# Low weight parts of layer 0's output projection on another engine, and two more pauses in the latent stream's routing

## The chip, the cores and the metric

The kernel runs on one core of a Trainium2 chip. A core has a matrix engine (TensorE, PE in the profile), a vector engine (VectorE, DVE), an activation engine (ScalarE, ACT), a general engine (GpSimd, POOL) and a queue engine that starts most DMAs (SyncE, SP). Each engine works through its own list of instructions in order; semaphores make one wait for another. The metric is device time in microseconds (us) of one execution, the median of several runs.

## The reference

The reference is a block of two layers for a stream x of 256 latent tokens and a stream ctx of 256 context tokens, each token 1024 wide, float32. Cut to what matters here, a layer is:

```python
x = x + g1 * merge_branches(attn_x, conv_x, pool_x, gate_x, lp)       # ... @ lp['w_out'] at its end
if not last:
    ctx = ctx + cg1 * merge_branches(attn_c, conv_c, pool_c, gate_c, lp)
x = x + g2 * expert_choice_ffn(modulate(rmsnorm(x, norm2_g[l]), sh2, sc2), w_router[l], ...)
if not last:
    ctx = ctx + cg2 * expert_choice_ffn(modulate(rmsnorm(ctx, ...), csh2, csc2), w_router[l], ...)

def expert_choice_ffn(h, w_router, w_gate, w_up, w_down):
    aff = softmax(h @ w_router)                    # 16 experts
    g, idx = top_k(transpose(aff), cap)            # each expert takes its 32 best tokens
    xe = h[idx]
    ye = (silu(xe @ w_gate) * (xe @ w_up)) @ w_down * g
    return zeros_like(h).at[idx].add(ye)
```

In layer 1, the last, only x goes on after the attention's keys and values.

## The kernel before

The work of a layer comes in two parts. The mixer (input projection, attention, convolution, pooling, three merges) ends with the merged sum m, eight pieces of 128x512 in layer 0 (both streams side by side) and of 128x256 in layer 1. Then come the output projection with w_out, the routing and the experts, whose weights, 2 MB at a time, fill nearly all of the DMA's time.

Products of this part keep float32 precision with two halves of each operand in the fast format: a high part h, rounded by ScalarE, and a low part, the rest, from a subtraction. `split` makes both for 128x1024 weights: `L238` is ScalarE's copy, `L239` the subtraction, which goes to VectorE for the letter "v" and to GpSimd for "p". The table `LOW` holds one letter per layer for each weight; for `wout` it is "pv": GpSimd in layer 0, VectorE in layer 1. The halves lie in the tile `ws`, of which there are two buffers here, so ScalarE can fill one only when TensorE is done with the one before the last.

`project(s)` forms stream s's output projection in ten steps: for each half of the columns four blocks of 12 products (`L872`: 4 of m's high part mh with the weights' high part, 4 of m's low part ml with it, 4 of mh with the weights' low part), and then the gate multiply (`L877`, VectorE) and the addition to the stream (`L879`: GpSimd for one of the four pieces, VectorE for three) with its squares (`L880`). The gates are first spread over the partitions by two products (`L853`). After each block and after each half it pauses (`yield`).

`route(s)` is the routing of stream s: products of the router with the first half of the columns (transposes `L895`, copies to `xT`, products `L904`), a pause, the second half, a pause; then the scale of the norm on GpSimd (`L909`, `L207`, `L208`), the logits' copy `lg` and transposes (`L915`), the softmax on VectorE and ScalarE (`L917` to `L931`), its transposes (`L934`), four rounds that find the eight largest values and strike them out (`L942`, `L943`), a pause; then the mask `mk`, the places of the chosen tokens by products with triangular matrices (`L954` to `L972`), the one-hot matrices S (`L965`, scaled by ScalarE in `L968`), and a last pause. Its tiles in the matrix accumulator come from a pool of four, `ax`.

`gather` multiplies a stream with S (`L987`) and so picks each expert's tokens (`xeT`). `L1080` is an expert's first pair of products, `L1103` and `L1108` its last, `L1125` the addition back.

The order of the work is set by these pauses: a loop runs one generator and lets another go on by one piece at each pause. In layer 0, x's routing starts after the sixth step of x's projection and goes on after its last; after that one piece of it follows each step of ctx's projection, and ctx's own routing starts after the sixth of those. The build's scheduler then places the instructions of each engine by that order and by priority; splits have a raised one, so they stand some steps ahead.

```python
        rt = route(0)
        for i, _ in enumerate(project(0)):
            if i == 5:
                next(rt)
        next(rt)
        rt1 = route(1) if NS == 2 else None
        if NS == 2:
            for i, _ in enumerate(project(1)):
                next(rt, None)
                if i == 5:
                    next(rt1)
```

Of the kernel before, what the change touches and what calls it, by code (L numbers as in the profile page):

```python
# [24 lines left out]


TAPS = dict(attn=(1, 4), pool=(4, 0), merge0=(8, 1), merge2=(9, 18))
LOW = dict(q="vv", k="pv", v="pv", cg="vv", ca="vv", pu="pv", g0="vv", g1="pv", g2="vp", wo="vv", wout="pv")
PSCALE = ("avaa", "aaaa")
MOD_EVERY = (1, 2)  # L30
MOD_AHEAD = 1
# [96 lines left out]
def dit_block(ctx: ExitStack, tc: tile.TileContext, out, kcv, kb16, rope_in, tok, cols, w_mod0, w_mod,  # L128
# [16 lines left out]
    def bank(tag, dt=F32):  # L145
        pool, bufs = psum[tag]
        return pool.tile([128, 512], dt, tag=tag, name=tag, bufs=bufs)
# [19 lines left out]
    def t2(name, n=512, dt=F32):  # L167
        return L.tile([128, n], dt, tag="t2", name=name, bufs=6)
# [42 lines left out]
    for l in range(DEPTH):  # L211
        last = l == DEPTH - 1
        NS = 1 if last else 2
# [256 lines left out]
        def pump_taps(n):  # L470
            for _ in range(min(n, len(taps))):
                ch, k = taps.popleft()
                if k == 0:
                    nc.vector.tensor_scalar(acc[:, ch], up[:, ch, :, 0:256], dw[:, ch:ch + 1],
                                            vec[:, VCB + 4 * l + ch:VCB + 4 * l + ch + 1],
                                            op0=ALU.mult, op1=ALU.add)
                else:
                    nc.vector.scalar_tensor_tensor(acc[:, ch], up[:, ch, :, k:k + 256],  # L478
                                                   dw[:, 4 * k + ch:4 * k + ch + 1], acc[:, ch],
                                                   op0=ALU.mult, op1=ALU.add)  # L480
# [20 lines left out]
        def unit(src, n, view="p (k n) -> p k n", eng="v", **kw):  # L501
            w = split(src, view, eng, **(kw or dict(k=8)))
            w = [v.rearrange("p (k n) -> p k n", k=8) for v in w]
            ps = bank("mm")
            mm3(ps[:, :n], w, (hh, hl), 8, n)
            nunit[0] += 1
            if nunit[0] % MOD_EVERY[l] == 0:
                pump_mod()
            return ps

        def win(c0):
            return load(w_in[l, c0 // 256], "p (k n) -> p k n", k=8)
# [20 lines left out]
        for u in range(2):  # L533
            tv = qw.pop() if qw else qload(u)
            for v in range(2):
                i = 2 * u + v
                ps = unit(tv[:, :, :, 64 * v:64 * v + 64], N, "p (k h n) -> p k h n",
                          LOW["q"][l], k=8, h=2)
                qx = t2("qx", N)
# [13 lines left out]
        kvw = win(OK_)  # L553
        ps = unit(kvw[:, :, 0:128], 512, eng=LOW["k"][l])
        kf = t2("kf")
        roped(kf[:, 0:256], ps)
        nc.scalar.activation(kf[:, 256:512], ps[:, 256:512], AF.Copy)
        for kv in range(2):
# [4 lines left out]
            nc.vector.tensor_sub(KL[ho, kv, :], kf[hp], KS[hp, kv, :].bitcast(F32))  # L563
        ps = unit(kvw[:, :, 128:256], 512, eng=LOW["v"][l])
        vf = t2("vf", 512)
# [93 lines left out]
        def sv(ap):  # L659
            return ap.rearrange("p (s n) -> p s n", s=NS)  # L660

        def conv_units():
            for u in range(2):
                wg_, wa_ = win(OG + 256 * u), win(OA + 256 * u)
                for v in range(2):
                    ch = 2 * u + v
                    ps = unit(wg_[:, :, 128 * v:128 * v + 128], N, eng=LOW["cg"][l])
                    th = t2("th", N)
                    nc.scalar.activation(th, ps[:, :N], AF.Tanh, scale=0.5)
                    yield  # L670
                    ps = unit(wa_[:, :, 128 * v:128 * v + 128], N, eng=LOW["ca"][l])
                    nc.vector.scalar_tensor_tensor(up[:, ch, :, CPAD:CPAD + 256], sv(th), 1.0,
# [30 lines left out]
        for u in range(2):  # L703
            wz = win(OP + 256 * u)
            for v in range(2):
                g = 2 * u + v
                w = POOLW[g]
                ps = unit(wz[:, :, 128 * v:128 * v + 128], N, eng=LOW["pu"][l])
                pump_taps(TAPS["pool"][l])
# [174 lines left out]
        def route(s):  # L884
# [25 lines left out]
            r = rms_scale(ss, 2)  # L910
            lg = t2("lg", 384)
            nc.vector.tensor_copy(lg, pl[:, 0:384])
            pt = bank("ax")
            for t in range(3):
                nc.tensor.transpose(pt[:, t * 128:(t + 1) * 128], lg[:, t * 128:(t + 1) * 128], ident)  # L915
# [13 lines left out]
            nc.vector.reduce_sum(sm, ex, axis=AX.X)  # L929
            nc.vector.reciprocal(sm, sm)  # L930
            nc.vector.tensor_mul(ex, ex, sm.unsqueeze(2).to_broadcast([128, 2, NE]))  # L931
            pa = bank("ax")
            for t in range(2):
                nc.tensor.transpose(pa[0:NE, t * 128:(t + 1) * 128], ex[:, t, :], ident)  # L934
# [62 lines left out]
        if last:  # L997
            prefetch(1)
# [8 lines that stand above are left out]
# [26 lines left out]
        for e in range(NE):  # L1033
# [36 lines left out]
            for i in range(4):  # L1070
                wg, wu = [eload().rearrange("p (k n) -> p k n", k=2) for _ in range(2)]
                for kk in range(2):
                    k = 2 * i + kk
# [126 lines left out]
```

## Time and profile before

| | us |
|---|---|
| median of 3 runs | 1696.55 (1694.93 to 1698.94) |
| profiled execution | 1699.61 |
| its span in the profile | 1697.8 |
| TensorE busy, of the span | 1469.8 |
| VectorE busy | 673.0 |
| ScalarE busy | 407.1 |
| GpSimd busy | 231.1 |

The DMA moves 530 MB in the span, 312 GB/s on the mean, and about 428 GB/s where it is full. In the chain of work that ended last, TensorE has 38% of the span, the DMA 27% and VectorE 4%.

### The profile page before, as it was taken

To read this page: it belongs to the slowest core of one execution; us is meant where nothing else is said; L and a number is where in the kernel's file an instruction comes from. 1 tells how busy PE (TensorE), PEld (TensorE's weight loads), DVE (VectorE), ACT (ScalarE), POOL (GpSimd) and SP (SyncE) were. 2 spreads that over 40 slices of the span, in tenths; PEclk is the share of its full clock that TensorE was granted. 3 is DMA by queue.
4 is the path that set the end of the run, shared out by engine and by line. 5 is a ranking of instruction groups with operands and counts; after the bars stand their busy time and mean duration, and the time that the engine had idled before them with its cause. 6 is when DMAs were issued, how large, how long until landed. Compare 5 with 4: busy or idle time off the path is not lost.

```text
span 1697.8 us, 19127 instructions
## 1 busy us (share of the span) xinstructions
PE 1469.8 (87%) x7788; PEld 797.6 (47%) x7788; DVE 673.0 (40%) x1141; ACT 407.1 (24%) x760; POOL 231.1 (14%) x234
## 2 busy tenths in 40 slices
PE   6999989999899999999988899999978656666575
PEld 2666667888654433333332377789843111111111
DVE  3589983441652221121211378966532110111011
ACT  3466212232432100100000258334421000000001
POOL 0301610254730000000000020225100000000000
PEclk9999999999999999999999999999989886887878
DMA  9644445243447999999999765665699999999995
GB/s 398 235 174 140 142 172 180 99 184 138 173 177 302 428 425 428 428 426 428 428 426 427 304 239 184 220 251 202 248 387 428 427 428 428 428 427 428 428 428 240
DMA packets 48185, 530.01 MB, mean 312 GB/s; under 512 B 5345, under 2 KB 6113, under 8 KB 7906
## 3 DMA queue, kind: packets, MB, share of 16 engines
q1 hardware_dynamic: 46224, 526.10, 76.2%
q10 hardware_dynamic: 1874, 2.70, 0.5%
q8 instruction: 61, 1.00, 0.2%
q14 instruction: 26, 0.21, 0.0%
HBM read 527.73 MB, written 1.05 MB: 311 GB/s over the span
## 4 chain that ended last, share of the span: by engine, by line
PE 38%; DMA 27%; DVE 4%; issue 2%; ACT 1%; POOL 1%; POOLq 0%; ACTq 0%; DVEq 0%; SPq 0%
DMA we<-in_w_e_dram 24%; PE mm L1080 11%; PE mm L1103 6%; PE mm L987 3%; PE mm L872 3%; PE mm L497 2%; PE mm L496 2%; PE mm L499 2%; DMA A<-in_w_e_dram 2%; PE ax L1125 2%; DVE acc L478 1%; PE mm L1108 1%; PE ax L1095 1%; PE md L255 1%; DVE ws L239 1%
## 5 line engine op out<-in xcount | busy, mean ns | idle before, releaser
L1080 PE MATMUL mm<-we,xeT 128*32 128x512 f32 (+1 forms) x1880 | 348.0, 662 | 99.5 <-DMA we<-in_w_e_dram 99.5
L1080 PEld LDWEIGHTS mm<-we,xeT 128*32 128x32 f32 (+1 forms) x1880 | 94.8, 129 | 342.2 <-issue 186.6
L496 PE MATMUL mm<-hh,ws 128*128 128x512 f32 (+1 forms) x672 | 222.8, 350 | 0.2
L497 PE MATMUL mm<-hl,ws 128*128 128x512 f32 (+1 forms) x672 | 219.7, 345 | 0.8 <-DVE hl L430 0.8
L238 ACT ACTIVATE ws<-w 128x1024 fp32r<-128x1024 f32 x132 | 139.4, 1058 | 301.0 <-PE mm L499 192.8
L1087 DVE TENSOR_TENSOR hm<-si,mm 64x512 f32<-64x512 f32 x48 | 33.1, 690 | 413.0 <-ACT si L1085 272.3
L1085 ACT ACTIVATE si<-mm 64x512 f32<-64x512 f32 x48 | 28.3, 590 | 686.7 <-PE mm L1080 686.7
L478 DVE SCALAR_TENSOR_TENSOR acc<-up,dw,acc 128x512 f32<-128x512 f32 (+1 forms) x240 | 154.5, 685 | 1.1
L239 DVE TENSOR_TENSOR ws<-w,ws 128x1024 fp32r<-128x1024 f32 x94 | 124.6, 1329 | 66.9 <-ACT ws L238 66.4
L496 PEld LDWEIGHTS mm<-hh,ws 128*128 128x128 f32 x672 | 128.3, 192 | 28.9 <-issue 12.6
L497 PEld LDWEIGHTS mm<-hl,ws 128*128 128x128 f32 x672 | 128.2, 191 | 18.6 <-issue 3.5
L499 PE MATMUL mm<-hh,ws 128*128 128x512 f32 (+1 forms) x672 | 132.5, 339 | 0.7 <-DVE ws L239 0.6
L239 POOL TENSOR_TENSOR ws<-w,ws 128x1024 fp32r<-128x1024 f32 x38 | 95.8, 2527 | 203.6 <-ACT ws L238 124.3
L1103 PE MATMUL mm<-we,hT 128*64 128x512 f32 x432 | 111.0, 637 | 4.8 <-ACT hT L1098 4.8
L499 PEld LDWEIGHTS mm<-hh,ws 128*128 128x128 f32 x672 | 107.2, 189 | 15.2 <-DVE ws L239 1.4
L1045 POOL COPY sel<-kc 48x128 f32<-48x128 f32 (+1 forms) x16 | 4.6, 285 | 798.2 <-DVE hm L1087 427.3
L1115 DVE TENSOR_TENSOR Y<-mm,G 32x512 f32<-32x512 f32 x64 | 44.0, 687 | 132.3 <-PE mm L1103 131.5
L1108 PE MATMUL mm<-we,hT 128*32 128x512 f32 x424 | 70.2, 779 | 9.4 <-DMA we<-in_w_e_dram 6.3
L1103 PEld LDWEIGHTS mm<-we,hT 128*64 128x64 f32 x432 | 33.6, 146 | 76.0 <-issue 65.3
L1125 PE MATMUL ax<-Y,sg 128*128 128x512 f32 x128 | 58.4, 603 | 8.8 <-DVE Y L1118 6.4
L1095 PE MATMUL ax<-kc,hm 64*128 64x64 f32 x192 | 32.6, 295 | 30.9 <-DVE hm L1087 30.2
L1118 DVE TENSOR_TENSOR Y<-mm,G 64x512 f32<-64x512 f32 x32 | 22.0, 689 | 94.0 <-PE mm L1108 93.6
(261 smaller groups left out, 1708.0 us busy)
## 6 DMA issues: line engine op xcount, KB each, us to landing
we<-in_w_e_dram SPq DMA_DIRECT2D x166, 2048.0 KB, 27.1
w<-in_w_mod_dram SPq DMA_DIRECT2D x44, 1024.0 KB, 5.4
w<-in_w_in_dram SPq DMA_DIRECT2D x42, 1024.0 KB, 4.8
A<-in_w_e_dram SPq DMA_DIRECT2D x20, 2048.0 KB, 23.8
w<-in_w_out_dram SPq DMA_DIRECT2D x12, 1024.0 KB, 4.9
we<-in_w_e_dram SPq DMA_DIRECT2D x10, 1024.0 KB, 17.2
wm<-in_w_mod_dram SPq DMA_DIRECT2D x4, 1024.0 KB, 19.1
w<-in_w_attn_o_dram SPq DMA_DIRECT2D x4, 1024.0 KB, 4.8
```

The costliest lines, as they stand in the source:

```text
L238: nc.scalar.activation(h, src, AF.Copy)
L239: (nc.gpsimd if eng == "p" else nc.vector).tensor_sub(lw, src, h.bitcast(F32))
L478: nc.vector.scalar_tensor_tensor(acc[:, ch], up[:, ch, :, k:k + 256], dw[:, 4 * k + ch:4 * k + ch + 1], acc[:, ch], op0=ALU.mult, op1=ALU.add)
L496: nc.tensor.matmul(ps, wh[:, k, :], ah[:, k, :n], start=k == 0, stop=False)
L497: nc.tensor.matmul(ps, wh[:, k, :], al[:, k, :n], start=False, stop=False)
L499: nc.tensor.matmul(ps, wl[:, k, :], ah[:, k, :n], start=False, stop=k == nk - 1)
L872: nc.tensor.matmul(pss[t], a, b, start=k == 0 and st == 0, stop=k == 7 and st == 2)
L987: nc.tensor.matmul(px, XS[s][:, t, paired(d)], Sv, start=t == 0, stop=t == 1)
L1080: nc.tensor.matmul(o, xeT[k // 4][:, k % 4, e, :], w[:, kk, 512 * f:512 * f + 512], start=k == 0, stop=k == 7)
L1103: nc.tensor.matmul(pd[64 * h:64 * h + 64, :], hT[:, 64 * k:64 * k + 64], rhs, start=k == 0, stop=k == 7)
L1108: nc.tensor.matmul(pd[o:o + 32, :], hT[:, c0:c0 + 32], rhs, start=k < 2, stop=k >= 6)
L1125: nc.tensor.matmul(po, sgs[s][:, t * 128:(t + 1) * 128], Y[:, s, cols], start=True, stop=True)
```

## The change

The letter for `wout` in layer 0 becomes "v", and `route` pauses twice more, after the copy of the logits and after the softmax. The two pauses hold only for a stream that is not the last of its layer (`s < NS - 1`): x in layer 0. In layer 1 there is one stream, so nothing moves there. The loop over `project(1)` is as before, so x's routing after its second pause now takes four steps of ctx's projection instead of two, each followed by a block of ctx's products.

```diff
-LOW = dict(q="vv", k="pv", v="pv", cg="vv", ca="vv", pu="pv", g0="vv", g1="pv", g2="vp", wo="vv", wout="pv")
+LOW = dict(q="vv", k="pv", v="pv", cg="vv", ca="vv", pu="pv", g0="vv", g1="pv", g2="vp", wo="vv", wout="vv")
...
             lg = t2("lg", 384)
             nc.vector.tensor_copy(lg, pl[:, 0:384])
+            if s < NS - 1:
+                yield
             pt = bank("ax")
...
             nc.vector.tensor_mul(ex, ex, sm.unsqueeze(2).to_broadcast([128, 2, NE]))
+            if s < NS - 1:
+                yield
             pa = bank("ax")
```

From here on a line in the changed program stands 2 lower after the first pause and 4 lower after the second. All 16 subtractions of layer 0's w_out leave GpSimd's list and stand in VectorE's. VectorE's list from the maximum of the softmax (`rmx`) to the first rounds of the top eight (`wk`), before:

```order
L924 TENSOR_REDUCE rmx<-rl_3427 128x2
L926 TENSOR_TENSOR rex<-rl_3427,rmx 128x32
L929 TENSOR_REDUCE rsm<-rex 128x2
L930 RECIPROCAL rsm<-rsm 128x2
L931 TENSOR_TENSOR rex<-rex,rsm 128x32
L942 MAX m_3444<-ax 16x8
L943 MATCH_REPLACE wk<-m_3444,ax 16x256
L942 MAX m_3444<-wk 16x8
```

The same place of VectorE's list in the changed program, where `ws` is a split's low part and `tmp` ctx's gate multiply:

```order
L239 TENSOR_TENSOR ws<-w,ws 128x1024
L926 TENSOR_REDUCE rmx<-rl_3442 128x2
L928 TENSOR_TENSOR rex<-rl_3442,rmx 128x32
L931 TENSOR_REDUCE rsm<-rex 128x2
L932 RECIPROCAL rsm<-rsm 128x2
L933 TENSOR_TENSOR rex<-rex,rsm 128x32
L239 TENSOR_TENSOR ws<-w,ws 128x1024
L946 MAX m_3476<-ax 16x8
L947 MATCH_REPLACE wk<-m_3476,ax 16x256
L877 TENSOR_TENSOR tmp<-mm,gb 128x512
L946 MAX m_3476<-wk 16x8
L239 TENSOR_TENSOR ws<-w,ws 128x1024
```

What stood in one piece is now laid between splits and gate multiplies; one more split, a gate multiply and two additions follow before the last round. TensorE's list from the transposes of the logits (`lg`) to those of the softmax (`rex`), before:

```order
L915 MATMUL ax<-kc,lg 128x128 x3
L872 MATMUL mm<-ws,mh 128x512 x2
L872 MATMUL mm<-ws,ml 128x512 x4
L872 MATMUL mm<-ws,mh 128x512 x4
L934 MATMUL ax<-kc,rex 16x128 x2
```

and the same place in the changed program:

```order
L917 MATMUL ax<-kc,lg 128x128 x3
L872 MATMUL mm<-ws,mh 128x512 x4
L872 MATMUL mm<-ws,ml 128x512 x4
L872 MATMUL mm<-ws,mh 128x512 x6
L938 MATMUL ax<-kc,rex 16x128 x2
```

There are 14 of ctx's products between the two where there were 10. TensorE's list from there to the transposes of the struck-out values (`wk`), before:

```order
L872 MATMUL mm<-ws,mh 128x512 x4
L872 MATMUL mm<-ws,ml 128x512 x4
L872 MATMUL mm<-ws,mh 128x512 x8
L872 MATMUL mm<-ws,ml 128x512 x4
L872 MATMUL mm<-ws,mh 128x512
L948 MATMUL ax<-kc,wk 128x16 x2
```

and in the changed program:

```order
L872 MATMUL mm<-ws,mh 128x512 x2
L872 MATMUL mm<-ws,ml 128x512 x4
L872 MATMUL mm<-ws,mh 128x512 x8
L872 MATMUL mm<-ws,ml 128x512 x4
L872 MATMUL mm<-ws,mh 128x512 x8
L872 MATMUL mm<-ws,ml 128x512 x4
L872 MATMUL mm<-ws,mh 128x512 x8
L872 MATMUL mm<-ws,ml 128x512 x2
L952 MATMUL ax<-kc,wk 128x16 x2
```

Here 40 products stand between, where 21 stood. The rest of x's routing, up to S, comes correspondingly later among ctx's products.

## Rows read from the trace of the kernel before

**Rows 1.** Stretches: length, busy PE, PEld, DVE, ACT, POOL, clock, DMA share, GB/s
```profile
424.50:455.20 30.70, 28.12 (x134) 20.05 (x133) 19.07 (x14) 14.42 (x22) 22.43 (x10) 1.00 0.63 240
455.20:490.60 35.40, 31.87 (x161) 22.83 (x160) 17.91 (x36) 13.87 (x23) 21.55 (x12) 0.95 0.30 99
...
501.00:517.40 16.40, 15.07 (x74) 8.38 (x75) 9.35 (x30) 6.25 (x16) 0.00 (x0) 1.00 0.00 2
...
560.00:788.00 228.00, 216.60 (x936) 78.16 (x938) 47.04 (x72) 18.02 (x33) 1.15 (x4) 0.96 1.01 427
```
**Rows 2.** Waits of the DMA queue SP, 490 to 560: total us, times, longest
```profile
SPq L355 <- PE mm L1080: 51.0, 8, 26.3
```
**Rows 3.** Chain that ended last, layer 0's experts: start, length
```profile
795.17 29.59 DMA we<-in_w_e_dram
```
**Rows 4.** TensorE in order of time: start, span; idle before in brackets
```profile
457.51 0.51 PE L895 MATMUL ax<-kc,xr 128*128 128x128 f32 x2 [0.83 <-POOL xr L879]
...
462.95 0.49 PE L915 MATMUL ax<-kc,lg 128*128 128x128 f32 x3
463.19 0.71 PE L872 MATMUL mm<-ws,mh 128*128 128x512 f32 x2
...
467.92 0.38 PE L934 MATMUL ax<-kc,rex 128*16 128x128 f32 x2 [2.17 <-DVE rex L931]
468.05 1.55 PE L872 MATMUL mm<-ws,mh 128*128 128x512 f32 x4
...
473.41 1.07 PE L872 MATMUL mm<-ws,ml 128*128 128x512 f32 x4
...
475.71 0.27 PE L972 MATMUL ax<-bt,mk 128*16 128x256 bf16 x1
...
481.40 0.99 PE L895 MATMUL ax<-kc,xc 128*128 128x128 f32 x6 [0.53 <-DVE xc L879]
...
489.72 1.07 PE L872 MATMUL mm<-ws,mh 128*128 128x512 f32 x4
490.63 1.88 PE L987 MATMUL mm<-S,xr 128*128 128x512 f32 x4
...
513.81 6.66 PE L1080 MATMUL mm<-we,xeT 128*64 128x512 f32 x30
```
**Rows 5.** GpSimd in order of time
```profile
441.60 2.38 POOL L239 TENSOR_TENSOR ws<-w,ws 128x1024 fp32r<-128x1024 f32 x1 [0.69 <-ACT ws L238]
```
**Rows 6.** VectorE in order of time; the last row is layer 1's
```profile
440.95 0.69 DVE L879 TENSOR_TENSOR xr<-xr,tmp 128x512 f32<-128x512 f32 x1
...
442.28 2.24 DVE L879 TENSOR_TENSOR xr<-xr,tmp 128x512 f32<-128x512 f32 x1
...
463.95 2.47 DVE L921 SCALAR_TENSOR_TENSOR rl<-rls,rstd 128x16 f32<-128x16 f32 x2
...
468.74 0.42 DVE L942 MAX8 m<-ax 16x8 f32<-16x256 f32 x1 [0.97 <-ACT slaff L937]
...
469.71 0.42 DVE L942 MAX8 m<-wk 16x8 f32<-16x256 f32 x1
...
499.36 0.38 DVE L921 SCALAR_TENSOR_TENSOR rl<-rls,rstd 128x16 f32<-128x16 f32 x2
...
1213.16 1.23 DVE L239 TENSOR_TENSOR ws<-w,ws 128x1024 fp32r<-128x1024 f32 x1 [1.49 <-ACT ws L238]
```
**Rows 7.** VectorE's groups by form, 424.5 to 490.6: busy us, mean ns
```profile
L827 DVE TENSOR_TENSOR ml<-A,mh 128x512 fp32r<-128x512 f32 x8 | 14.0, 1805 | 6.8 <-ACT mh L826 6.8
```
**Rows 8.** Stretches again: layer 1's output projection of x
```profile
1204.70:1230.70 26.00, 26.00 (x134) 19.91 (x132) 14.82 (x20) 11.85 (x20) 0.78 (x1) 1.00 0.63 264
```
**Rows 9.** Stretches again: behind the softmax
```profile
469.40:471.10 1.70, 1.70 (x5) 1.32 (x4) 1.58 (x5) 0.00 (x0) 1.12 (x1) 0.50 0.00 0
```
**Rows 10.** ScalarE in order of time
```profile
476.51 1.06 ACT L238 ACTIVATE ws<-w 128x1024 fp32r<-128x1024 f32 x1 [2.72 <-PE mm L872]
477.47 1.32 ACT L968 ACTIVATE S<-S,rstd 128x512 f32<-128x512 f32 x2
```

## The prediction

> **What bounds the kernel now.** I read the stretches first, since the change touches one place: the end of layer 0's mixer. From 424.5 to 490.6 us TensorE forms the output projection of both streams and the first routing; from there to 513.8 it gathers tokens; then the experts start. The reader is to see three things. In the two stretches of the projection (424.5 to 455.2 the latent stream x, 455.2 to 490.6 the context stream ctx with x's routing laid between) TensorE is the engine with the most work, 28.1 of 30.7 and 31.9 of 35.4 us, and the DMA is not full [rows 1]. From 501.0 to 517.4 the DMA moves nothing: the expert buffers are filled, and the queue waits, up to 26.3 us at a time, for an expert product to free one [rows 1, 2]. From 560 on it is full, and later the chain consists of waits for expert weights, such as 29.6 us at 795 [rows 1, 3]. So layer 0 ends when a full DMA stream ends, but that stream starts when TensorE begins its first expert, at 513.81 [rows 4]. Whatever the projection gains should move the stream, and all behind it, by the same amount. The order of the DMAs on SP is the same before and after.
>
> **The change part by part.** Durations are those of the profiled execution, 1699.61 us (span 1697.8 and 1.8 around it); the runs shown have a median of 1696.55, 3.06 lower, and I take the gain off that.
>
> *Low parts of w_out on VectorE.* The change takes 16 subtractions of 128x1024 off GpSimd, 2.38 us each when undisturbed [rows 5], and adds 16 to VectorE, where layer 1 already does them at 1.23 us [rows 6]: 19.7 us on top of the 37.0 (19.07 + 17.91) that VectorE is busy in the two stretches [rows 1]. But part of the 37.0 is waiting inside instructions. While GpSimd subtracts from 441.60 to 443.98, VectorE's add at 442.28 takes 2.24 us, where the same form at 440.95 takes 0.69; a 128x16 multiply-add pair at 463.95 takes 2.47, against 0.38 for the other stream's pair at 499.36 [rows 5, 6]; and the eight subtractions on the merged sum take 1.8 us on average [rows 7]. With GpSimd out of the way that gives back 8 x (1.8 - 0.69) = 8.9 us, 1.6 at the add and 2.1 at the pair, so VectorE ends near 44 us of work in some 58.
>
> For x's products I need no model, because layer 1 has the same program there: one stream, the same products, the same interleaving of the first half of the routing, and the low parts on VectorE. That stretch takes 26.0 us with TensorE busy in all of it [rows 8], against 30.7 here [rows 1]: **4.7 us**. What differs is that the merged sum's subtractions are 128x512 here, twice layer 1's size. If half of each of the 8 lay on the path, 8 x 0.35 = 2.8 us, only 1.9 would be gained; I keep that as the low end. They should be hidden: the later ones are first needed in the third block of 12 products, 24 x 0.227 = 5.4 us after the first (0.227 is the step from 489.72 to 490.63 over four products [rows 4]).
>
> *ctx's products with x's routing between, and the two pauses.* Before, TensorE passes from the logits' transposes at 462.95 over 10 products to the transposes of the softmax at 467.92, for which it waits 2.17 us [rows 4]. The chain between, from the end of the first transposes, is 4.5 us. Without the blocked pair it is 2.1 shorter; with the one split that now stands in it on VectorE it is 1.23 longer: 3.6. The first pause gives 14 products as cover, 3.2 us, and a change-over of 0.1, so 0.3 of the 2.17 stays: 1.9 gained. Behind that wait the granted clock is 0.50 (the 1.2 GHz level) from 469.4 to 471.1 [rows 9], and the 16 products from 468.05 to 473.41 take 5.36 us instead of 16 x 0.227 = 3.6 [rows 4]; less a change-over, 1.6 is gained if the clock stays. The wait of 0.83 at 457.51 left it at 1.00 up to 468 or so, so 0.3 should leave it too; that wait itself, for GpSimd's add on x, I leave as it is. The wait of 0.53 at 481.40 is for an add on ctx that a GpSimd split had blocked; it goes: 0.5 gained. Together 4.0.
>
> Against that stand three costs. The second pause lays 40 products (9.1 us) between the softmax's transposes and those of the top-8 result, where 21 lay. But on VectorE the four rounds of MAX8 and MATCH_REPLACE8, 0.97 each (468.74 to 469.71) [rows 6], now have three splits (3.7) and three gate operations of 0.69 between them: 3.9 + 3.7 + 2.1 = 9.7. I charge 0.5. TensorE changes between products and transposes some two times more, 0.1 each (two products after transposes take 0.71 at 463.19, where 0.39 + 0.23 is the bare time): 0.2. And the one-hot matrix S, ready at 478.8 for a gather at 490.63 [rows 4, 10], loses nearly all of its 12 us of lead. From the last mask product (475.98) S took 2.8 us; in the new order 10 products (2.3) and 24 small routing products and transposes stand between, over 4 us in all. I charge nothing; a late S would cost what is missing, 1 us or so. The stretch then gives 4.0 - 0.7 = **3.3 us**, between 0 and 5.5.
>
> The sum is 4.7 + 3.3 = **8.0 us**: 1691.6 against the profiled execution, 1688.6 against the median. GpSimd keeps two adds and the norm's scale, so its own queue holds up nothing new. The stretch from 490.6 to 513.8 has the same instructions as before and no split in it.
>
> One rule weighs against part of this. The add at 442.28 shows the later of the two engines held until the other's instruction is over [rows 5, 6]. The Trainium skill ("SBUF — State Buffer", section "SBUF: two separate sides") states that the port pair which VectorE and GpSimd share is an exclusive lock, that it goes to whichever starts first, and that a VectorE operation with two SBUF inputs takes it; the trace agrees with 2.24 against 0.69. By that rule VectorE's splits can now hold GpSimd's remaining add on x, which TensorE awaits at 457.51, by up to 1.23 us: the time would be 1689.8.
>
> **The rivals.** (a) *Only x's stretch gains.* VectorE serves the routing and the splits in one order, so ctx's stretch wins as much as it loses: 4.7, time 1691.9. For it: the top-k chain of 9.7 against 9.1. Against it: the 2.17 wait and the slow clock behind it have a cause that goes. (b) *The weights' stream takes it back*: 1696.5. For it: the DMA is full from 560 on and has the chain's longest parts. Against it: it is idle for 16 us first, waiting for this very TensorE. (c) *Slower: VectorE's order.* There are six places, from the logits to the mask, where a split stands behind a routing instruction that waits for TensorE or ScalarE, while only two split buffers exist. If at each TensorE had to wait for a whole split, 1.06 on ScalarE [rows 10] and 1.23 on VectorE, it would lose 6 x 2.29 = 13.7, so 13.7 - 8.0 = 5.7 us slower: 1702.3. It decides from 8.0 / 6 = 1.3 us at each place. Against it: the low half is needed only after 8 of a block's 12 products, 1.8 us after the high half, and in layer 1 VectorE stands idle 1.49 us for ScalarE before a split while TensorE is never late [rows 6, 8]. (d) *All small waits go*, also the top-k's, the one at 457.51 and the change-overs: 10.5 us, 1686.0.
>
> **How the numbers follow.** The forecast (a gain of 6 to 10) gets 0.66, (a) with 3 to 6 0.16, (b) 0.08, (c) 0.05, (d) 0.05. A gain of 10.5 with 0.5 for the spread of a median gives 1685.5; the low end of x's stretch with 0.6 from ctx's, a gain of 2.5, gives 1694.0. About 0.2%, 3.4 us, is what a measurement tells from no change. Of (a) 0.13 lies beyond it: faster 0.66 + 0.05 + 0.13 = 0.84, same 0.03 + 0.08 = 0.11, slower 0.05.
>
> **What would show it.** In the profile after: x's stretch 26 us long with VectorE's splits at 1.23; no VectorE add above 1 us there; a wait for the softmax under 0.5 and the granted clock at 1.00 throughout; the gather beginning near 482.6 and the first expert near 505.8; the DMA's idle stretch before it, and the expert stretch, as long as now. A split that comes late at several blocks, a gather waiting for S, or a first expert that comes earlier without the end moving would make the prediction wrong.

## The result, and the profile after

| | before | after |
|---|---|---|
| median of the runs made for the comparison | 1697.18 (1694.93 to 1700.23, 5 runs) | 1688.83 (1687.23 to 1690.28, 5 runs) |
| profiled execution | 1699.61 | 1690.28 |
| its span | 1697.8 | 1688.5 |

The changed kernel takes 0.9945 of the time before, with a 95% interval of 0.9932 to 0.9957: faster by 0.55% by this ratio, while the two medians differ by 8.3 us (0.49%). 1688.6 was predicted, between 1685.5 and 1694.0. A later run of the same changed kernel, in another comparison, gave 1691.34 against 1700.00, again 0.9945 [0.9934, 0.9957].

The stretches of the output projection (length, then busy time of PE, PEld, DVE, ACT and POOL with instruction counts, granted clock, DMA share, GB/s), and part of the DMA's idle stretch behind it. The first begins with the first product of the projection (`L853`), the second with the gate multiply that follows x's last product (`L877`; 455.20 us before, 450.74 after), and the second ends at the gather:

```profile
424.69:450.74 26.05, 26.05 (x133) 20.12 (x132) 19.08 (x23) 14.40 (x22) 1.68 (x1) 1.00 0.74 282
450.74:482.21 31.47, 30.81 (x162) 22.00 (x161) 21.70 (x43) 13.97 (x23) 2.37 (x4) 1.00 0.45 158
505.00:508.00 3.00, 3.00 (x17) 1.20 (x17) 0.41 (x1) 1.77 (x3) 0.00 (x0) 1.00 0.00 0
```

Beside [rows 1]: cut at the same events, x's stretch went from 30.68 (424.52 to 455.20) to 26.05 us, which is layer 1's length [rows 8], ctx's from 35.43 (to 490.63) to 31.47. GpSimd's 44 us of work in the two stretches has become 4. VectorE has 15 of the 16 splits more in them (the first runs ahead of them, at 423.31) and yet only 40.8 us of work against 37.0. Those 15 splits take 18.8 us, so everything else takes 22.0 instead of 37.0: some 15 us of its time before was waiting inside instructions. The prediction had found 12.6 of them and put VectorE at 44 us; two more additions had been held before, of 1.48 and 2.17 us.

In x's stretch before, TensorE waited at these places (the shorter waits left out):

```profile
431.93 2.14 PE L872 MATMUL mm<-ws,mh 128*128 128x512 f32 x8 [0.95 <-POOL ws L239]
...
435.29 0.73 PE L872 MATMUL mm<-ws,ml 128*128 128x512 f32 x2 [0.76 <-DVE ml L827]
...
444.57 1.11 PE L895 MATMUL ax<-kc,xr 128*128 128x128 f32 x7 [0.60 <-DVE xr L879]
```

The second and third are for VectorE operations that had been held, the first is for a GpSimd split itself. In x's stretch part of the gain can therefore be that a low part no longer comes late from GpSimd; in ctx's stretch TensorE waited for no split. After the change TensorE has none of these waits.

TensorE in order of time (start, span, in brackets the idle time ahead and what ended it); a line carries its new number, 2 or 4 higher:

```profile
452.84 0.50 PE L895 MATMUL ax<-kc,xr 128*128 128x128 f32 x2 [0.56 <-POOL xr L879]
...
461.30 0.49 PE L917 MATMUL ax<-kc,lg 128*128 128x128 f32 x3
...
465.10 0.39 PE L938 MATMUL ax<-kc,rex 128*16 128x128 f32 x2
465.24 0.71 PE L872 MATMUL mm<-ws,mh 128*128 128x512 f32 x2
...
474.55 0.29 PE L952 MATMUL ax<-kc,wk 16*128 16x16 f32 x2
...
482.21 1.88 PE L991 MATMUL mm<-S,xr 128*128 128x512 f32 x4
484.27 0.51 PE L895 MATMUL ax<-kc,xc 128*128 128x128 f32 x2 [0.18 <-POOL xc L879]
```

The waits of 2.17 us for the softmax and 0.53 us for `xc` [rows 4] are gone, that for `xr` is 0.56 instead of 0.83, and the gather stands at 482.21 instead of 490.63. VectorE, where the same pieces ran:

```profile
429.10 3.09 DVE L827 TENSOR_TENSOR ml<-A,mh 128x512 fp32r<-128x512 f32 x5
...
440.49 0.69 DVE L879 TENSOR_TENSOR xr<-xr,tmp 128x512 f32<-128x512 f32 x1
...
452.06 1.81 DVE L239 TENSOR_TENSOR ws<-w,ws 128x1024 fp32r<-128x1024 f32 x1 [0.63 <-ACT ws L238]
...
462.30 0.38 DVE L923 SCALAR_TENSOR_TENSOR rl<-rls,rstd 128x16 f32<-128x16 f32 x2
462.59 1.22 DVE L239 TENSOR_TENSOR ws<-w,ws 128x1024 fp32r<-128x1024 f32 x1
```

The subtractions on the merged sum take 0.82 us on the mean instead of 1.8 [rows 7], the blocked add and the blocked pair of [rows 6] 0.69 and 0.38, the splits 1.22, but for the one at 452.06: 1.81. GpSimd beside it:

```profile
451.51 1.28 POOL L879 TENSOR_TENSOR xr<-xr,tmp 128x512 f32<-128x512 f32 x1 [24.02 <-DVE tmp L877]
```

Behind the projection everything moves as one. The gather comes 8.42 us earlier, the first expert 8.40 (505.41 against 513.81 [rows 4]), the last scatter of layer 0 8.20 (954.59 against 962.79), the first product of layer 1's projection 7.97 (1196.71 against 1204.68). The SP queue's longest wait for an expert buffer is 26.3 us as before [rows 2]. By layer 1's first expert the two profiled executions differ by one further microsecond, most of it in layer 1's unchanged routing: a stretch of it lasts 9.20 us at a granted clock of 0.81 before, 8.60 at 0.99 after. The change has no instruction there, so I do not count it.

### The profile page after: what moved, and what is told of

It reads as the page before. It is cut to its first block, busy times and chain, and to the rows that moved or that the text cites. A ratio compares the mean times of both kernels' runs of the same rounds, so it can differ in the third digit from the quotient of the medians.

```text
span 1688.5 us, 19114 instructions
## 1 busy us (share of the span) xinstructions
PE 1458.6 (86%) x7788; PEld 795.5 (47%) x7788; DVE 677.4 (40%) x1157; ACT 407.1 (24%) x760; POOL 189.9 (11%) x218
## 5 line engine op out<-in xcount | busy, mean ns | idle before, releaser
L239 DVE TENSOR_TENSOR ws<-w,ws 128x1024 fp32r<-128x1024 f32 x110 | 144.5, 1317 | 80.7 <-ACT ws L238 80.2
L239 POOL TENSOR_TENSOR ws<-w,ws 128x1024 fp32r<-128x1024 f32 x22 | 54.3, 2473 | 180.0 <-ACT ws L238 98.1
```

Of the source, the lines that this page charges most:

```text
L239: (nc.gpsimd if eng == "p" else nc.vector).tensor_sub(lw, src, h.bitcast(F32))
```

## The experiments

The ratios are to the kernel before, run on the same chip. The start named in them is the first product of the projection (`L853`), 424.52 us before and 424.69 after.

**The letter alone, and the pauses alone.** The first is the kernel before with the new letter, the second the changed kernel with the old one.

```diff
 first:  -LOW = dict(..., wo="vv", wout="pv")
         +LOW = dict(..., wo="vv", wout="vv")
 second: the reverse edit, made on the changed kernel
```

> The kernel before with wout="vv" alone; no pauses. Theory A, as in the prediction (the pauses give the softmax and the top-k chain their cover): x's stretch takes 26.0 us, but ctx's stretch keeps 1 to 3 us of its waits, so 1690 to 1692. Theory B (the scheduler moves ctx's products by itself once the splits are on VectorE; between the logits' and the softmax's transposes TensorE's list has 18 products here against 14 with the pauses and 10 before): ctx's stretch 31.5 us as with the whole change, 1688.8, and the two pauses are worth nothing.

> The changed kernel with wout="pv" again: the two pauses alone, layer 0's low parts on GpSimd. Theory of the held engine (VectorE's operations with two SBUF inputs wait for a GpSimd split to end): x's stretch stays at 30.7 us, its subtractions at 1.8 us mean; in ctx's stretch the scale pair of the softmax is still held for up to 2.4 us, 12 products cover instead of 10, so the wait for the softmax falls only from 2.2 to 1.7 or so; gain 0 to 2 us, 1695 to 1697. Rival (the pauses were the main gain of ctx's stretch): gain 3 us or more there, 1694 or less.

The letter alone: 1689.85 us, 0.9953 [0.9938, 0.9969]; from the start to the gather 57.37 us, against 57.52 with the pauses and 66.11 before. The pauses alone: 1697.23 us, 0.9989 [0.9979, 1.0]; 64.42 us. The time of the letter alone lies between the two theories (1690 to 1692 and 1688.8) and decides nothing; its stretch, as short as with the pauses, speaks for the second. So the letter is the whole change, and beside it the pauses are worth nothing that can be measured. TensorE with the letter alone:

```profile
460.36 0.49 PE L915 MATMUL ax<-kc,lg 128*128 128x128 f32 x3
460.61 0.48 PE L872 MATMUL mm<-ws,ml 128*128 128x512 f32 x1
460.93 2.01 PE L872 MATMUL mm<-ws,mh 128*128 128x512 f32 x8
462.78 1.07 PE L872 MATMUL mm<-ws,ml 128*128 128x512 f32 x4
463.68 1.29 PE L872 MATMUL mm<-ws,mh 128*128 128x512 f32 x5
464.95 0.39 PE L934 MATMUL ax<-kc,rex 128*16 128x128 f32 x2
```

Without any pause 18 products stand between the two transposes, where 10 stood before and 14 stand with the pauses: the scheduler had filled the place by itself as soon as the letter changed. With the pauses alone the hold on VectorE only moves to another instruction of the softmax, of 128x32 (VectorE, then TensorE, then the stretches behind TensorE's two waits):

```profile
466.65 0.38 DVE L923 SCALAR_TENSOR_TENSOR rl<-rls,rstd 128x16 f32<-128x16 f32 x2
467.07 0.19 DVE L926 TENSOR_REDUCE rmx<-rl 128x2 f32<-128x32 f32 x1
467.29 2.19 DVE L928 TENSOR_TENSOR rex<-rl,rmx 128x32 f32<-128x32 f32 x1
```
```profile
470.45 0.39 PE L938 MATMUL ax<-kc,rex 128*16 128x128 f32 x2 [1.55 <-DVE rex L933]
...
478.81 0.29 PE L952 MATMUL ax<-kc,wk 16*128 16x16 f32 x2 [0.88 <-DVE wk L947]
```
```profile
470.45:478.00 7.55, 7.47 (x33) 5.84 (x33) 5.89 (x14) 3.52 (x7) 5.35 (x3) 1.00 0.41 138
478.81:484.00 5.19, 5.19 (x45) 3.65 (x46) 2.60 (x6) 2.67 (x4) 1.62 (x2) 1.00 0.88 357
```

The reader is to see a subtraction of the shortest kind at 2.19 us, where its like takes 0.19 in the changed kernel. The softmax's wait shrinks from 2.17 to 1.55, and a new one of 0.88 appears at the top-8 result. The granted clock behind both is 1.00.

**Does the gain pass through to the end?** 44 products whose result nothing reads, before the first gather.

```diff
+        if NS == 2:
+            px = bank("mm")
+            for i in range(44):
+                nc.tensor.matmul(px, mh[:, i % 8, 0:128], mh[:, i % 8, 0:512], start=i == 0, stop=i == 43)
```

> The changed kernel with 44 more products of 128x512, whose result nobody reads, on TensorE between ctx's projection and the gather: 44 x 0.227 = 10.0 us. Theory (layer 0's weight stream starts when TensorE's first expert starts, so all behind moves by as much): first expert and end both 10 us later, 1698.8. Rival (the full DMA stream takes up part of a shift): the first expert 10 later, the end less than 5 later, below 1694.

1698.67 us, 1.0 [0.9991, 1.0008]. The block lasts 10.17 us in the profile; from the start to the first expert the stretch is 9.8 us longer than in the changed kernel (90.48 against 80.72), and the whole loses 0.55% or 9.3 us, all that the change had won. So between this place and the end hardly anything gives time back, though the DMA is full for most of layer 0's experts.

**Is it GpSimd's work beside VectorE that costs?** Four subtractions of 128x1024 on GpSimd, laid beside the top-8 rounds; they write x's part of `ml`, which is not needed any more, and no engine waits for them: GpSimd's next instruction comes 13 us after their end.

```diff
+                dead = ml[:, 0:4, 0:256].rearrange("p k (a b) -> p k a b", b=16)
+                for _ in range(4):
+                    nc.gpsimd.tensor_sub(dead, dead.bitcast(F32),
+                                         ex[:, 0, :].unsqueeze(1).unsqueeze(1).to_broadcast([128, 4, 16, 16]))
```

> The changed kernel with four subtractions of 128x1024 on GpSimd, two SBUF inputs, written into a part of a tile that is no longer read, started when the softmax is done; nothing on the path waits for them. Theory (the two engines hold each other up): VectorE's splits (1.23 us) and adds (0.69) beside them take up to 2.4 us longer each, the top-k chain, which has under 0.5 us to spare, ends 3 to 7 us later, and TensorE waits for it: 1692 to 1696. Rival (what the change won is only that a low part takes 1.2 instead of 2.4 us): these four are off every path, 1688.8.

1698.07 us, 0.9996 [0.9987, 1.0006]: 0.51% over the change, 8.7 us. GpSimd, then VectorE, then TensorE and the stretch behind its wait:

```profile
464.95 11.86 POOL L938 TENSOR_TENSOR ml<-ml,rex 128x1024 fp32r<-128x1024 f32 x4 [7.89 <-DVE rex L933]
```
```profile
465.48 2.95 DVE L239 TENSOR_TENSOR ws<-w,ws 128x1024 fp32r<-128x1024 f32 x1 [0.68 <-ACT ws L238]
468.35 0.41 DVE L950 MAX8 m<-ax 16x8 f32<-16x256 f32 x1
...
469.21 0.67 DVE L877 TENSOR_TENSOR tmp<-mm,gb 128x512 f32<-128x512 f32 x1
469.80 0.41 DVE L950 MAX8 m<-wk 16x8 f32<-16x256 f32 x1
...
472.10 2.49 DVE L879 TENSOR_TENSOR xc<-xc,tmp 128x512 f32<-128x512 f32 x1
...
475.36 2.52 DVE L239 TENSOR_TENSOR ws<-w,ws 128x1024 fp32r<-128x1024 f32 x1
```
```profile
479.25 0.39 PE L956 MATMUL ax<-kc,wk 16*128 16x16 f32 x2 [4.83 <-DVE wk L951]
```
```profile
479.20:483.40 4.20, 4.15 (x16) 2.99 (x17) 1.83 (x3) 0.72 (x2) 0.00 (x0) 0.50 0.37 82
```

Splits of 1.23 take up to 2.95, an add of 0.69 takes 2.49. GpSimd's four take 2.97 us each instead of 2.4, so it is held as well. Not held are the gate multiply `L877`, whose first input `mm` lies in the matrix accumulator (0.67), and MAX8 (0.41). TensorE, which has no part in these four instructions, then waits 4.83 us for the top-8 result, and behind that wait the granted clock is 0.50, the 1.2 GHz level, for 4.2 us. The expectation of 3 to 7 us had left out that second part; the rival, that GpSimd's splits had only been late, falls for this place, since here none was late. For x's stretch, where TensorE did wait 0.95 us for a GpSimd split before, no run parts the two.

**The last add of x on GpSimd.** All additions `L879` on VectorE.

```diff
-                    (nc.gpsimd if nh == 1 and t == 0 else nc.vector).tensor_add(xs, xs, tmp)
+                    nc.vector.tensor_add(xs, xs, tmp)
```

> The changed kernel with GpSimd's adds of the gated projection on VectorE too (one of four pieces of each stream and layer). Theory (a two-input operation is shorter on VectorE, 0.69 against 1.27 us, and nothing is held): the wait of 0.56 us for this add in x's stretch goes, the 1.90 in layer 1's first routing falls by 0.7; about 1 us in all, 1688. Rival (VectorE's order: the add then stands ahead of a split and of the second gate multiply, and what waited for GpSimd waits for VectorE instead): no change, or up to 1 us slower.

1689.92 us, 0.9939 [0.9926, 0.9953]: not to be told from the change. The stretch from the start to the gather is 56.92 us, 0.6 shorter, about the wait of 0.56, which is gone. In layer 1, where 0.7 was expected, TensorE's wait of 1.90 for this add became two for VectorE's adds, 1.29 and 0.82, so nothing came of it.

**The letter for x's products only.** x's splits on VectorE, ctx's on GpSimd.

```diff
-                               LOW["wout"][l], k=2)
+                               "p" if l == 0 and s == 1 else "v", k=2)
```

> The changed kernel with low parts of w_out on VectorE for x's products and on GpSimd for ctx's. If the two stretches gain apart from each other: x's stretch 26.0 us, ctx's as with the pauses alone, 33.7, so a gain of 4.7 + 1.7 = 6.4, 1691. If most of the gain depended on the whole letter: less than 4.

1692.75 us, 0.996 [0.9946, 0.9975], by the ratio 6.8 us less than before; from the start to the gather 59.81. So some 6.3 of the 8.6 us that this stretch gains come with x's letter (the two pauses are in this kernel too), 2.3 with ctx's. With ctx's letter back on GpSimd, TensorE's waits for the softmax (1.54) and the top-8 result (0.90) are those of the pauses alone.

**The other letters.** If a GpSimd split costs VectorE more than it spares it, the five other "p" in the table should pay as well. First all of them, then the pooling branch (`pu`) alone, then the others without it, and then all of them with the 20 additions of the pooled sums (`L721`) too.

```diff
-LOW = dict(q="vv", k="pv", v="pv", cg="vv", ca="vv", pu="pv", g0="vv", g1="pv", g2="vp", wo="vv", wout="vv")
+LOW = dict(q="vv", k="vv", v="vv", cg="vv", ca="vv", pu="vv", g0="vv", g1="vv", g2="vv", wo="vv", wout="vv")
...
-                    nc.gpsimd.tensor_add(nxt[:, :, lo2:hi2], cur[:, :, lo2 - a:hi2 - a],
+                    nc.vector.tensor_add(nxt[:, :, lo2:hi2], cur[:, :, lo2 - a:hi2 - a],
```

> The changed kernel with every remaining split off GpSimd as well (k, v, pool and third merge of layer 0, second merge of layer 1). Theory (moving a split pays only where TensorE waits and VectorE has room): TensorE is busy all the time from 240 to 424 us, so nothing is won there, and in the pool branch, where VectorE is busy 39 of 40 us, four splits more cost up to 4 x 1.23 = 5 us; 1688 to 1694. Rival (GpSimd's splits hold VectorE wherever they run, so every one moved pays): 1687 or less.

> The changed kernel with one more letter: the four splits of the pooling branch's weights in layer 0 go from GpSimd to VectorE, all others stay. Theory (their four holds of the convolution's VectorE work are what moving all letters won in layer 0): the output projection begins near 417.5 us instead of 424.69, the rest follows rigidly, 1681.8 us, ratio to before 0.990. Rival (the attention's two splits, or the second gate's, carry it): the projection begins at 424 or later, 1688 us, ratio 0.994 to 0.995. A second rival, half and half: 1685, ratio 0.992.

> The complement: all letters on VectorE but the pooling branch's in layer 0. Theory: layer 0's projection begins near 424.7 us as in the changed kernel, and only layer 1's mixer gains, some 3.8 us from the third gate's eight splits: 1685 us, ratio 0.9922. Rival (the other letters carry layer 0's gain): the projection begins near 417.5, 1678 us, ratio 0.988.

> All letters on VectorE, as before in the run with all of them, and also the 20 additions of the pooled sums, 0.64 to 2.7 us each on GpSimd. Theory (a two-input GpSimd operation on SBUF holds VectorE for its length, so that it costs more than the work moved): VectorE is held less by 12 to 15 us in layer 0's mixer and gets 10 additions of about 0.7 us more; 2 to 5 us come off the run with all letters, 1674 to 1677 us, ratio 0.985 to 0.986. Rival (VectorE is 94% busy between 150 and 250 us, so moved work adds itself): 7 us slower than that run, 1686 us, ratio 0.992.

The times are medians of three comparisons, so the ratios compare better than they do.

| | us | ratio | projection starts | layer 1, last scatter before it to its projection |
|---|---|---|---|---|
| the change | 1688.83 | 0.9945 [0.9932, 0.9957] | 424.69 | 242.12 |
| all letters | 1678.77 | 0.9873 [0.9859, 0.9888] | 417.29 | 238.36 |
| pooling branch only | 1684.03 | 0.9918 [0.9901, 0.9935] | 417.29 | 243.83 |
| the others only | 1686.41 | 0.9928 [0.9912, 0.9943] | 424.71 | 238.24 |
| all letters and pooled additions | 1670.98 | 0.9839 [0.9821, 0.9857] | 413.54 | 234.01 |

For all letters I had expected no gain; that was wrong. The table tells where it comes from: the pooling branch's four splits carry all of layer 0's 7.4 us, the others 3.8 us in layer 1. Layer 0's splits of `k`, `v` and `g1` bring nothing at its projection (424.71), so not every split that is moved pays. (The totals of the two halves sum to less than the whole; parts that none of these edits touches differ by 2 us between these executions, so the starts tell more than the totals. By its total the pooling branch alone, 0.9918, is nearer to the forecast for "half and half" than to the 0.990 of the theory; its start, 417.29, is what speaks for the theory.) The pooled additions take off another 0.34%, or 5.8 us; the two intervals leave some 2 to 10, so the total does not tell whether it was more than the 2 to 5 us forecast. At the two starts of the table they bring 3.75 and 4.35 us. The stretch from 150 to 250 us, of the change, of all letters, and with the pooled additions:

```profile
150.00:250.00 100.00, 91.57 (x430) 61.99 (x430) 96.47 (x132) 31.63 (x55) 37.32 (x42) 0.98 0.43 149
```
```profile
150.00:250.00 100.00, 98.14 (x463) 67.23 (x463) 94.01 (x138) 33.71 (x57) 23.88 (x38) 0.98 0.44 152
```
```profile
150.00:250.00 100.00, 100.00 (x482) 69.70 (x482) 93.91 (x149) 33.79 (x57) 7.29 (x28) 1.00 0.48 166
```

VectorE does more instructions in each (132, 138, 149) and is busy for less time; TensorE's idle time there goes from 8.4 to 1.9 to nothing. VectorE's convolution steps, from 180 to 225 us, in the same order of kernels:

```profile
L478 DVE SCALAR_TENSOR_TENSOR acc<-up,dw,acc 128x512 f32<-128x512 f32 x35 | 35.3, 1064 | 0.0
```
```profile
L478 DVE SCALAR_TENSOR_TENSOR acc<-up,dw,acc 128x512 f32<-128x512 f32 x38 | 30.8, 866 | 0.0
```
```profile
L478 DVE SCALAR_TENSOR_TENSOR acc<-up,dw,acc 128x512 f32<-128x512 f32 x36 | 25.5, 749 | 0.0
```

The same instruction takes 1064, 866 and 749 ns on the mean: the 96% were in part time held. The last version is the fastest of all, 1.6% under the kernel before and 1.1% under the change.

## Why the prediction was right, and where it was not

**x's stretch, 4.7 us: right, by its own comparison: 4.6.** It became 26.05 us, and layer 1's, cut at the same events, is 26.04 (1204.68 to 1230.72). The low end, with the merged sum's subtractions on the path, did not come: seven of the eight take 0.6 to 0.7 us, one, beside a GpSimd multiply, 1.79.

**ctx's stretch, 3.3 us: 4.0 to the gather** (from 450.74 to 482.21, 31.47 against 35.43), a little more than its sum. Of the wait for the softmax, where 0.3 was to stay, none shows; the clock is 1.00 throughout, and the wait for `xc` is gone. The 0.5 charged for the top-8 rounds was not needed: VectorE struck out the last values at 474.50, TensorE's transposes stood at 474.55 with no wait. The margin is 0.05 us, so that nothing was paid here is partly luck. These two, 0.3 and 0.5, are about what the sum fell short by. S was ready at 479.86 for a gather at 482.21, so most of its lead was lost and 2.3 us stayed.

**The step that failed: "The first pause gives 14 products as cover."** The number of products is right, what brought them is not. With the letter alone the scheduler puts 18 there, and the same gain comes without a pause; with the pauses alone 1.7 of 8.6 us come. The sum was right because the step credited the right cover to the wrong edit. The listing compared before with the whole change only, and a listing of each part would have shown it.

**The weighed rule on the shared port: right in kind, wrong in direction.** I let VectorE's splits hold GpSimd's add on x. GpSimd came first (451.51 against 452.06) and took its usual 1.28; the split was held, 1.81 instead of 1.23. The rest is as the Trainium skill ("SBUF — State Buffer", section "SBUF: two separate sides") states it: a VectorE operation with two SBUF inputs and a GpSimd operation that reads SBUF exclude one another for a whole instruction. The traces agree, with 0.69 against 2.24 and 2.49, and in its exception too: the multiply that reads the accumulator is not held (0.67).

**The rivals.** Only x's stretch gains (1691.9): no, ctx's gave 4.0. The weights' stream takes it back (1696.5): no; 8.4 us arrive at the first expert and 8.2 at layer 0's last scatter, and the 44 products pass through in the other direction. VectorE's order (1702.3): TensorE waits in none of the six places; the split that stands ahead of the softmax's maximum ends at 463.81, 1.3 us before its transposes. All small waits go (1686.0): 0.56 stays, and the experiment that takes it away wins too little to be told.

**Not foreseen** was how far the reason reaches. I called VectorE's busy time "waiting inside instructions" for this stretch only; between 150 and 250 us the same profile shows it 96% busy with GpSimd at 37%, and the same edit there wins 7.4 us more at the projection's start.

## What to carry to other kernels

When VectorE and GpSimd both work on SBUF, compare the durations of one form of VectorE instruction: if the mean lies well above the shortest, the busy share is partly waiting, and moving GpSimd's work to VectorE can make both the work and the time shorter, even at 96% busy. It does not pay everywhere: layer 0's splits of `k`, `v` and `g1` were moved too and brought its projection no earlier. What looks like an engine's help must be priced by what it holds up, not by what it does. And where a scheduler orders the instructions, list each part of a change alone before crediting one of them with the place it fills.

## What the runs showed of the hardware

A GpSimd subtraction of 128x1024 (2.4 us alone) can cost VectorE almost its whole length even on a small instruction: one of 128x32 took 2.19 us instead of 0.19. Four of them, 11.86 us of GpSimd's time that no engine waited for, cost the kernel 8.7 us, of which part lay in TensorE's granted clock: 0.50 for 4.2 us behind a wait of 4.83. The waits of 1.55 and 0.88 left it at 1.00, the one of 2.17 before the change did not [rows 4, 9]. Whether the length of the wait alone decides that, no run here tells. MAX8 and the multiply that reads the accumulator kept their durations beside GpSimd's work (0.41 and 0.67).

The last version gains 3.75 us at the projection's start over the one with all letters, but 6.6 at layer 0's last scatter; where the other 2.8 us come from is open. The stretch from layer 0's first expert to its last scatter, which none of the edits touches, lasts 446.4 us there and 448.3 to 451.3 in the profiles of all the other versions.
